# A hybrid encoder layer: another order inside the turns of its recurrence, and an order point for the first loads of the out projection

## The chip, the cores and the metric

The kernel runs on one core of one Trainium2 chip. The metric is the device time of one execution in microseconds (us). Three executions of the kernel before took 2543.28, 2548.71 and 2551.45 us; their median is 2548.71 us. A fourth execution was profiled, and all rows quoted here are from it.

The engines are named as in the profile: PE multiplies matrices (PEld loads its weights), ACT applies functions and copies out of the accumulator banks, DVE does element-wise arithmetic, POOL does smaller arithmetic, and SP only issues transfers.

## The reference, cut to what matters

One layer on x (2048 tokens, width 1024) and 256 memory tokens, all in float32, each step wrapped in RMS norms and added to a residual:

```python
z = u @ w_in                       # 2816 columns: 768 for attention, 4 x 512 for the recurrence
ya = swa_with_sinks(qa, ka, va)    # sliding window attention, 8 heads
yh = hgrn2(qh, fh, ih, gh)         # gated recurrence, 4 heads of 128 x 128 state
y  = concat(ya, yh) @ w_out        # the out projection
...
y  = cross_attention(u, m, wq_x, wk_x, wv_x, wo_x)
...
y  = (silu(u @ w_gate) * (u @ w_up)) @ w_down
```

The recurrence, chunk by chunk (64 tokens), is

```python
A     = (qc * exp(b - b_mid)) @ (kc * exp(b_mid - b)).T      # causal part within the chunk
o     = A @ vc + (qc * exp(b)) @ S_prev                      # plus what the state gives
S     = exp(b_last) * S_prev + (kc * exp(b_last - b)).T @ vc # the state for the next chunk
out   = rms_norm(o) * silu(g)
```

so the output of a chunk needs the state from before it, and the state from chunk to chunk is the only chain through time.

## The kernel before, in words

Every float32 product is made of three products of split operands (hi*hi, hi*lo, lo*hi), so each weight or activation tile is loaded raw by a transfer, split by ACT (hi) and DVE (lo), and then used by PE.

The layer runs in stages. First z is made for the first 1024 tokens. Then, in one stretch (`mix`), three strands run beside each other: the rest of the input projection, the attention, and the recurrence (`hgrn`). After that the *fold* (`fold_cross`) multiplies the cross attention's weights together ahead of time: eight steps for the keys, eight for the queries, eight for the values (`wv_x`, read in columns), and eight for the output weight (`wo_x`, read in rows). The eight `wo_x` tiles are numbered j = 0 to 7; each has 512 KB and feeds 12 matmuls of 512 columns into four accumulator banks, and two of them (one head) make two result tiles that go to `vo_d`. The raw tiles of the fold (`raw`) have three buffers. The last eight pairs of the recurrence run interleaved with the fold, two fold steps to a turn. Then come the blocked products of the rest of the layer (`phases`): the out projection (operand `y_d`), the scores, the values and the feed-forward part. Each of their blocks loads its operand as two tiles `sraw` of 512 KB, for which there are four buffers; block 0 of the out projection is the first.

The recurrence handles 128 tokens (a pair of chunks) with four helpers. `hgrn_front(n)` loads k, q and v of pair n, makes the masked A in one of two buffers `atz`, the scaled queries q6, and the transposes kt and vt. `hgrn_state` multiplies kt and vt and adds the decayed old state: POOL multiplies (L924), DVE adds (L925), into one of two buffers W. `hgrn_out` multiplies A by vt (L934) and the old W by q6 (L935), squares on ACT (L939), takes the root on POOL and scales on DVE (L944); it also loads the gate `sg`. `hgrn_last` transposes (L952), multiplies with the gate (L953) and stores to `y_d`. `hgrn` deals these out in turns; a turn handles the front of one pair and the rest of earlier ones.

What order the engines get: the program is traced in the order of the Python code, and a planner then plays it against a model of the engines at compile time, giving each engine, whenever it is free, the earliest traced instruction that is ready in that model. The order so found is fixed for each engine; on the chip each engine takes its instructions in that order and waits at each for its inputs. SP likewise issues its transfers one after the other. The buffers of one tag are given out in the order in which the program first writes them. `self.queued(ins)` adds a rule to the planner: what is traced inside on the engine of `ins` goes behind `ins` in that engine's order. It adds no wait. `self.traced(engine)` is the instruction traced last on an engine.

`phases` is a generator; the fold stage steps it nine times, which brings the first tiles T of the out projection's weights (loads into tiles named z, splits into T). Its tenth step calls `stream(0)`, which traces the two loads of block 0's operand (`sraw<-y_d`) and then yields. In the kernel before, this tenth step is part of the plain loop at the end of `mix`.

Of the kernel before, what the change touches and what calls it, by code (L numbers as in the profile page):

```python
# [48 lines left out]
class Layer:  # L49
# [79 lines left out]
    def raw_tile(self):  # L129
        self._n += 1  # L130
        return self.wp.tile([P, D], F32, tag="raw", name=f"raw_{self._n}", bufs=3)
# [62 lines left out]
    def mix(self):  # L194
        tc, I = self.tc, self.I
        kw = dict(reuse_waits="tile")
        with contextlib.ExitStack() as left:
# [40 lines left out]
            phases = self.phases(self.jobs(), None, lambda: self.io_tile("z"))  # L238
# [25 lines left out]
            with (  # L264
                tc.tile_pool(name="t3", bufs=3, **kw) as self.ts,
                tc.tile_pool(name="t4", bufs=3, **kw) as self.tb,
                tc.tile_pool(name="s3", bufs=2, side="right", **kw) as self.st_pool,
                contextlib.ExitStack() as at,
            ):
                self.banks(at, "ps3", **MOST)  # L270
                self.raws = 4
                for _ in phases:
                    pass

# [8 lines left out]
    def fold_cross(self):  # L283
# [10 lines left out]
        def split_tiles():  # L294

            if next(turn) % 3 < 2:
                return self.split_tiles()
            self._n += 1
            return [ph.tile([P, D], F32R, tag=f"w{x}", name=f"w{x}_{self._n}") for x in ("hi", "lo")]
# [18 lines left out]
        for t in range(M // P):  # L318
            m = raw_tile()
# [6 lines left out]
        for d in range(KT):  # L326
# [6 lines left out]
            o = self.io_tile("x")  # L333
# [12 lines left out]
        for h in range(4):  # L346
            banks = [[self.bank(k) for k in "sh"] for _ in range(2)]
            for i in range(2):
                j = 2 * h + i
                raw = raw_tile()  # L350
                self.load(raw, self.I["wo_x"][j * P:(j + 1) * P, :])
                wh, wl = split_tiles()
                self.split(raw, wh, wl, "A")
                for mt in range(2):
                    ms = slice(mt * P, (mt + 1) * P)
                    ah, al = vT[0][:, j, ms], vT[1][:, j, ms]
                    for q in range(2):
                        sl = slice(q * 512, (q + 1) * 512)
                        nc.tensor.matmul(banks[mt][q], ah, wh[:, sl], start=(i == 0), stop=False)
                        nc.tensor.matmul(banks[mt][q], ah, wl[:, sl], start=False, stop=False)  # L360
                        nc.tensor.matmul(banks[mt][q], al, wh[:, sl], start=False, stop=(i == 1))
                if i == 0:
                    yield
            for mt in range(2):
                o = self.io_tile("x")
                for q in range(2):
                    nc.scalar.activation(o[:, q * 512:(q + 1) * 512], banks[mt][q], AF.Copy)
                self.store(self.vo_d[(2 * h + mt) * P:(2 * h + mt + 1) * P, :], o)
            yield
# [547 lines left out]
    def hgrn_state(self, n, kinds, kt, vt):  # L917
        nc, ph = self.nc, self.hg
        prev = self.W
        W = self.W = ph.tile([P, 4, P], F32, tag="W", name=f"W{n}", bufs=2)  # L920
        ps = self.bank(kinds[0])
        for h in range(4):
            nc.tensor.matmul(ps[:, h * P:(h + 1) * P], kt[:, h, :], vt[:, h, :], start=True, stop=True)
        nc.gpsimd.tensor_tensor(W, prev, self.G[:, n, :, 1].unsqueeze(2).broadcast_to([P, 4, P]), ALU.mult)  # L924
        nc.vector.tensor_tensor(W, ps.rearrange("p (h t) -> p h t", h=4), W, ALU.add)  # L925

    def hgrn_out(self, n, kinds, q6, at, vt, W):
        nc, ph = self.nc, self.hg
# [28 lines left out]
    def hgrn(self, pairs, kinds):  # L957

        f, o = {}, {}
        for n in itertools.chain(pairs, (None, None)):  # L960
            if o:
                l, v = o.popitem()
                self.hgrn_last(l, kinds, *v)
            if f:
                m, (q6, at, kt, vt) = f.popitem()
                o[m] = self.hgrn_out(m, kinds, q6, at, vt, self.W)
                self.hgrn_state(m, kinds, kt, vt)
            if n is not None:
                f[n] = self.hgrn_front(n, kinds)
            yield  # L970

    def swa(self, pairs, kinds):
# [826 lines left out]
```

## Time and profile before

| | |
|---|---|
| median of three executions | 2548.71 us |
| the profiled execution: its time | 2551.48 us |
| the profiled execution: span of the program | 2549.8 us |
| PE busy in the span | 2504.8 us (98%) |
| DVE, ACT, POOL busy | 1794.9, 1261.8, 372.7 us |
| transfers | 482.13 MB, mean 189 GB/s |
| recurrence beside the fold and the input projection | about 600 to 730 us |
| last fold steps (`wo_x`) | 748 to 772 us |

The profile gives, for one execution, the start and length of each instruction, what it waited for, the clock that PE was granted (PEclk, 1.00 is full), and the transfers. A row of the timeline has start and length in us, engine, line, operation, output<-inputs, shapes, count, and in brackets the idle time just before it with what ended it. A row of a table by stretches gives for each engine the busy time and the instructions in the stretch, then the clock, the mean busy share of the 16 transfer engines and GB/s.

### The profile page before, as it was taken

What the parts mean: (1) busy time and instruction counts of PE and PEld (TensorE: products, weight loads), DVE (VectorE), ACT (ScalarE), POOL (GpSimd) and SP (SyncE); (2) the same over time, 40 slices, a digit from 0 to 9 for tenths busy, and PEclk for the clock granted to TensorE, in tenths of its full rate; (3) what the DMA queues carried; (4) which work ended last, traced back from release to release, by engine and by line L of the source; (5) the groups of instructions that cost most, each with busy time, mean ns of one, the idle gap of its engine ahead of it and who ended that gap; (6) DMA issues with size and microseconds to landing.
All of it is one profiled execution on the core that took longest, in us unless ns stands there. A gap on an engine that the chain in (4) does not pass through costs nothing.

```text
span 2549.8 us, 34301 instructions
## 1 busy us (share of the span) xinstructions
PE 2504.8 (98%) x12006; PEld 2094.9 (82%) x12006; DVE 1794.9 (70%) x2871; ACT 1261.8 (49%) x2635; POOL 372.7 (15%) x540
## 2 busy tenths in 40 slices
PE   9999999999999999999999999999999999999998
PEld 8878888888987778878878888888888888888886
DVE  8885588986466989887876655576566557574766
ACT  5553467664565566566753333353333335443543
POOL 4331334331301111102200000000000000000022
PEclk9999999999999999999999999999999999999999
DMA  6455645773887996866964522254566434565886
GB/s 200 148 166 178 187 146 152 219 233 101 263 296 265 319 328 192 268 206 220 331 209 140 182 91 84 75 206 143 163 207 198 142 118 160 177 191 106 229 174 154
DMA packets 379437, 482.13 MB, mean 189 GB/s; under 512 B 22016, under 2 KB 274944, under 8 KB 379264
## 3 DMA queue, kind: packets, MB, share of 16 engines
q1 hardware_dynamic: 373216, 457.92, 56.1%
q0 software_dynamic: 6048, 22.02, 5.1%
q8 instruction: 94, 1.54, 0.2%
q14 instruction: 79, 0.65, 0.1%
HBM read 313.14 MB, written 166.72 MB: 188 GB/s over the span
## 4 chain that ended last, share of the span: by engine, by line
PE 80%; DVE 7%; DMA 6%; ACT 3%; issue 3%; POOL 1%; SPq 1%; DVEq 0%; POOLq 0%; ACTq 0%
PE psm L1137 22%; PE psm L1139 22%; PE psm L1138 22%; PE psg L158 2%; PE psg L157 2%; PE psg L156 2%; DVE T L996 1%; DMA h1t_d<-row 1%; DVE S L996 1%; ACT junk L1512 1%; DMA raw<-in_wv_x_dram 1%; SPq L75 1%; DVE row L1406 1%; DVE sum L1112 0%; DMA qd<-z_d 0%
## 5 line engine op out<-in xcount | busy, mean ns | idle before, releaser
L1137 PE MATMUL psm<-T,S 128*128 128x512 f32 x2680 | 1034.7, 391 | 14.3 <-ACT part L1152 7.8
L1138 PE MATMUL psm<-T,S 128*128 128x512 f32 x2680 | 1043.0, 390 | 4.0 <-DVE T L996 3.9
L1139 PE MATMUL psm<-T,S 128*128 128x512 f32 x2680 | 1030.1, 390 | 4.4 <-DVE S L996 4.4
L1137 PEld LDWEIGHTS psm<-T,S 128*128 128x128 f32 x2680 | 503.5, 188 | 127.6 <-ACT part L1152 12.9
L1139 PEld LDWEIGHTS psm<-T,S 128*128 128x128 f32 x2680 | 503.5, 188 | 111.1 <-DVE S L996 6.6
L1138 PEld LDWEIGHTS psm<-T,S 128*128 128x128 f32 x2680 | 503.5, 188 | 110.0 <-DVE T L996 6.8
L993 ACT ACTIVATE S<-sum 128x512 fp32r<-128x512 f32 (+1 forms) x370 | 223.5, 619 | 378.1 <-PE psm L1139 276.3
L996 DVE TENSOR_TENSOR S<-sraw,S 128x512 fp32r<-128x512 f32 (+1 forms) x315 | 211.2, 678 | 212.4 <-ACT S L993 209.2
L1152 ACT ACTIVATE part<-psm 128x512 f32<-128x512 f32 x285 | 168.6, 596 | 249.5 <-PE psm L1139 231.6
L996 DVE TENSOR_TENSOR S<-sum,S 128x512 fp32r<-128x512 f32 (+1 forms) x388 | 257.2, 673 | 42.0 <-ACT S L993 38.3
L993 ACT ACTIVATE S<-sraw 128x512 fp32r<-128x512 f32 (+1 forms) x300 | 185.0, 618 | 113.1 <-PE psm L1139 110.3
L1545 POOL DMA_DIRECT2D y_d<-row x16 | 14.0, 877 | 1077.7 <-DVE row L1729 1026.8
L996 DVE TENSOR_TENSOR T<-row,T 128x1024 fp32r<-128x1024 f32 (+1 forms) x112 | 131.0, 1182 | 30.8 <-ACT T L993 28.7
L156 PE MATMUL psg<-u,whi 128*128 128x512 f32 x320 | 127.1, 397 | 0.8 <-DVE z L724 0.8
L158 PE MATMUL psg<-u,wlo 128*128 128x512 f32 x320 | 126.9, 397 | 0.0
L157 PE MATMUL psg<-u,whi 128*128 128x512 f32 x320 | 126.6, 396 | 0.0
L1512 ACT ACTIVATE junk<-row 128x512 f32<-128x512 f32 x160 | 99.5, 623 | 40.3 <-DVE row L1534 17.4
L993 ACT ACTIVATE T<-row 128x1024 fp32r<-128x1024 f32 (+1 forms) x112 | 113.3, 1031 | 5.7 <-DMA row<-d_s 3.5
L1680 DVE TENSOR_TENSOR row<-psm,part 128x512 f32<-128x512 f32 x66 | 43.7, 687 | 66.5 <-PE psm L1139 66.4
L1689 DVE TENSOR_TENSOR part<-psm,part 128x512 f32<-128x512 f32 x66 | 43.8, 687 | 60.5 <-PE psm L1139 60.3
L996 DVE TENSOR_TENSOR wlo<-raw,whi 128x1024 fp32r<-128x1024 f32 x44 | 53.8, 1223 | 44.6 <-ACT whi L993 29.5
L1729 DVE TENSOR_TENSOR row<-psm,part 128x512 f32<-128x512 f32 x72 | 49.1, 687 | 49.4 <-PE psm L1139 49.3
(362 smaller groups left out, 3584.7 us busy)
## 6 DMA issues: line engine op xcount, KB each, us to landing
sraw<-in_w_gate_dram SPq DMA_DIRECT2D x44, 512.0 KB, 3.9
sraw<-in_w_up_dram SPq DMA_DIRECT2D x44, 512.0 KB, 3.9
hid_d<-row SPq DMA_DIRECT2D x44, 512.0 KB, 2.7
sraw<-hid_d SPq DMA_DIRECT2D x32, 512.0 KB, 4.3
sraw<-in_w_in_dram SPq DMA_DIRECT2D x44, 256.0 KB, 3.8
z_d<-pair SPq DMA_DIRECT2D x20, 512.0 KB, 3.6
raw<-in_w_in_dram SPq DMA_DIRECT2D x20, 512.0 KB, 5.4
z_d<-z SPq DMA_DIRECT2D x20, 512.0 KB, 4.1
```

The lines of the kernel that those rows point to most:

```text
L156: nc.tensor.matmul(ps, ah, bh, start=(i == 0), stop=False)
L157: nc.tensor.matmul(ps, ah, bl, start=False, stop=False)
L158: nc.tensor.matmul(ps, al, bh, start=False, stop=(i == n - 1))
L993: self.nc.scalar.activation(hi, raw, AF.Copy)
L996: self.nc.vector.tensor_tensor(lo, raw, f32(hi), ALU.subtract)
L1137: nc.tensor.matmul(ps, s[:, 0, k, :], t[:, 0, k, :], start=st, stop=False, **kw)
L1138: nc.tensor.matmul(ps, s[:, 0, k, :], t[:, 1, k, :], start=False, stop=False, **kw)
L1139: nc.tensor.matmul(ps, s[:, 1, k, :], t[:, 0, k, :], start=False, stop=sp, **kw)
L1152: nc.scalar.activation(t, ps, AF.Copy)
L1512: self.nc.scalar.activation(junk, a, AF.Square, scale=float(D) ** -0.5, accum_out=to)
L1689: nc.vector.tensor_tensor(c, a, c, ALU.add)
L1729: nc.vector.tensor_tensor(d, a, b, ALU.add)
```

## The change

Two edits. In `hgrn`, a turn was traced as last (of pair l), output and state (of pair m), front (of pair n); now it is state (m), front (n), last (l), output (m). The output still uses the state from before pair m: `hgrn_state` returns it. Second, the tenth step of `phases` is taken inside `self.queued(self.folded)`, where `self.folded` is the load of the third `wo_x` tile (j = 2): the two loads of block 0's operand go behind that load in SP's order.

```diff
@@ mix
                 self.banks(at, "ps3", **MOST)
                 self.raws = 4
+                with self.queued(self.folded):
+                    next(phases)
                 for _ in phases:
                     pass
@@ fold_cross
                 raw = raw_tile()
                 self.load(raw, self.I["wo_x"][j * P:(j + 1) * P, :])
+                if j == 2:
+                    self.folded = self.traced(mybir.EngineType.SP)
                 wh, wl = split_tiles()
@@ hgrn_state
         nc.vector.tensor_tensor(W, ps.rearrange("p (h t) -> p h t", h=4), W, ALU.add)
+        return prev
@@ hgrn
         for n in itertools.chain(pairs, (None, None)):
+            if f:
+                m, (q6, at, kt, vt) = f.popitem()
+                W = self.hgrn_state(m, kinds, kt, vt)
+            else:
+                m = None
+            if n is not None:
+                f[n] = self.hgrn_front(n, kinds)
             if o:
                 l, v = o.popitem()
                 self.hgrn_last(l, kinds, *v)
-            if f:
-                m, (q6, at, kt, vt) = f.popitem()
-                o[m] = self.hgrn_out(m, kinds, q6, at, vt, self.W)
-                self.hgrn_state(m, kinds, kt, vt)
-            if n is not None:
-                f[n] = self.hgrn_front(n, kinds)
+            if m is not None:
+                o[m] = self.hgrn_out(m, kinds, q6, at, vt, W)
             yield
```

## The prediction, made before the result was known

> **What bounds the kernel now.** I read the page first, then the table by stretches over the part that the edits touch, then the list of PE's waits there, and last the timelines of SP, ACT, DVE and PE around the one wait that stands out.
>
> ```profile
> span 2549.8 us, 34301 instructions
> PE 2504.8 (98%) x12006; PEld 2094.9 (82%) x12006; DVE 1794.9 (70%) x2871; ACT 1261.8 (49%) x2635; POOL 372.7 (15%) x540
> 300.00:600.00 300.00, 296.03 (x1663) 253.97 (x1662) 259.58 (x627) 192.67 (x550) 100.32 (x156) 0.99 0.58 177
> 600.00:744.00 144.00, 143.07 (x1105) 137.42 (x1103) 75.49 (x109) 75.29 (x180) 35.30 (x44) 1.00 0.75 229
> 744.00:754.00 10.00, 6.16 (x21) 4.54 (x21) 6.13 (x9) 4.79 (x7) 0.00 (x0) 0.83 0.89 311
> 754.00:800.00 46.00, 46.00 (x202) 37.73 (x201) 18.38 (x20) 25.84 (x45) 2.53 (x3) 1.00 0.79 291
> 800.00:1300.00 500.00, 483.53 (x2154) 394.22 (x2153) 441.48 (x640) 313.70 (x698) 84.68 (x130) 1.00 0.84 269
> ```
>
> PE is the bound everywhere: it idles 2549.8 - 2504.8 = 45.0 us in the whole span. The edits leave PE's work as it is, so they can only win idle time, or add some. The recurrence runs between 300 and 730 us, where PE idles 300 - 296.03 = 3.97 us and 144 - 143.07 = 0.93 us. The ten microseconds from 744 stand out: 3.84 us idle and a clock of 0.83. Behind them, to 800 us, PE has no gap.
>
> ```profile
> 748.01 0.50 PE L359 MATMUL pss<-whi,kv 128*128 128x512 f32 x1 [3.54 <-ACT whi L993]
> 749.27 0.79 PE L360 MATMUL pss<-wlo,kv 128*128 128x512 f32 x1 [0.29 <-DVE wlo L996]
> 746.91 1.06 ACT L993 ACTIVATE whi<-raw 128x1024 fp32r<-128x1024 f32 x1 [1.80 <-DMA raw<-in_wo_x_dram]
> 736.25 10.58 DMA raw<-in_wo_x_dram
> 733.47 2.69 SPq L75 DMA_DIRECT2D sraw<-y_d  x4
> 736.25 4.86 SPq L75 DMA_DIRECT2D raw<-in_wo_x_dram  x3
> 743.77 1.58 SPq L75 DMA_DIRECT2D sraw<-y_d  x2
> 749.25 3.06 SPq L75 DMA_DIRECT2D raw<-in_wo_x_dram  x3
> 748.00:750.00 2.00, 1.69 (x5) 1.12 (x6) 1.95 (x2) 1.82 (x3) 0.00 (x0) 0.73 0.71 262
> 750.00:752.00 2.00, 2.00 (x7) 1.52 (x5) 1.96 (x3) 0.52 (x1) 0.00 (x0) 0.50 0.80 258
> 752.00:754.00 2.00, 2.00 (x9) 1.64 (x8) 0.00 (x0) 0.49 (x1) 0.00 (x0) 0.91 0.91 234
> ```
>
> The reader is to see a queue. PE waits 3.54 us for the first split of `wo_x`; that split waits for its load; the load was issued at 736.25 and took 10.58 us. Just ahead of it SP issued four `sraw<-y_d` of 512 KB (blocks 0 and 1 of the out projection), which nobody uses on PE before the fold ends at 772. Then the clock: it is at 0.50 to 0.91 while PE starts again, and the time lost is 2 x (0.27 + 0.50 + 0.09) = 1.72 us. The gap thus costs 3.54 + 0.29 + 1.72 = 5.55 us.
>
> **The change, part by part: the order point.** Both loads of block 0 go behind the third `wo_x` load. Buffers of one tag are given out in traced order, so block 1's and block 2's loads can't overtake block 0's: all six move, and with them 2 MB that stood ahead of the first `wo_x` tile. When are the three `wo_x` loads issued then? Each needs a raw buffer, freed by a split of `wv_x` on DVE.
>
> ```profile
> 734.36 1.22 DVE L996 TENSOR_TENSOR wlo<-raw,whi 128x1024 fp32r<-128x1024 f32 x1
> 735.91 1.23 DVE L996 TENSOR_TENSOR wlo<-raw,whi 128x1024 fp32r<-128x1024 f32 x1
> 739.52 1.23 DVE L996 TENSOR_TENSOR wlo<-raw,whi 128x1024 fp32r<-128x1024 f32 x1 [2.06 <-ACT whi L993]
> 738.43 1.06 ACT L993 ACTIVATE whi<-raw 128x1024 fp32r<-128x1024 f32 x1 [2.29 <-DMA raw<-in_wv_x_dram]
> 748.18 1.06 ACT L993 ACTIVATE whi<-raw 128x1024 fp32r<-128x1024 f32 x1 [0.21 <-DMA raw<-in_wo_x_dram]
> 744.00:748.00 4.00, 0.47 (x4) 0.27 (x3) 2.22 (x6) 1.96 (x3) 0.00 (x0) 1.00 1.03 399
> raw<-in_wo_x_dram SPq DMA_DIRECT2D x1, 512.0 KB, 4.0
> 752.39 0.39 PE L359 MATMUL psh<-whi,kv 128*128 128x512 f32 x1
> 752.62 0.39 PE L359 MATMUL pss<-whi,kv 128*128 128x512 f32 x1
> ```
>
> The splits end at 735.58, 737.14 and 740.75, so the first tile's load moves only from 736.25 to about 735.6. What moves more is its landing: nothing but the last `wv_x` tile is ahead of it, which lands by 738.43. A `wo_x` load issued without a queue took 4.0 us (the one of 749.25), and a full queue moves 399 GB/s, 524 KB in 1.31 us, also the step between the splits of the first two tiles (746.91, 748.18). So tile 0 lands at 735.6 + 4.0 = 739.6, tile 1 at 737.2 + 4.0 = 741.2, tile 2 at 740.8 + 4.0 = 744.8. ACT and DVE need about 1.06 + 1.23 us: tile 0 is split by 742. PE finishes the last `wv_x` product at 744.47 (0.47 us busy in the stretch from 744) and goes on at once: the 5.55 us go.
>
> What is late next is tile 3. SP issues the four `y_d` loads from 741.2 to 743.9 (2.69 us, as now), and tile 3 right behind; they land 1.31 us apart: 746.1, 747.4, 748.7, 750.0, and tile 3 at 751.3. Its halves are ready at 752.4 (hi) and 753.6 (lo). PE is there at 744.47 + 3 x 12 x 0.23 = 752.8, and starts with three hi products (0.7 us). So it just fits; tile 4 has its buffer free about 744 and lands one step later. The moved loads are themselves due by 772 and land by 750; their splits on ACT (0.63 us each) now fall among those of tiles 2 to 5 and the copies out of the banks. I put 0.5 us on that. Bounds: nothing lost (5.55 won) to the gap come back whole ahead of tile 3 (0 won); I take 5.0, near the upper end, because tile 3's row of sums fits without help. Blocks 1 and 2 have 20 us of cover and cost nothing; without it each late operand would cost its 1.31 us.
>
> **The turns.** Written out as a sequence, the order was last, output, state, front and is the same cycle after, begun at another place; no instruction is added. What changes is the distance: between the front of a pair and its output now lies a whole further turn, and between an output and the next state and front, which reuse its W, `atz`, q6 and vt buffers, nearly nothing where a turn lay.
>
> ```profile
> L924 POOL TENSOR_TENSOR W<-W,G 128x512 f32<-128x512 f32 x14 | 15.5, 1108 | 28.5 <-DVE W L925 26.7 <-DMA vr<-z_d 1.8
> L925 DVE TENSOR_TENSOR W<-psg,W 128x512 f32<-128x512 f32 x8 | 5.5, 688 | 9.2 <-PE psg L923 9.2
> PE pst L850 <- DVE w_mn L821: 0.9, 1, 0.9
> PE psg L156 <- DVE z L724: 0.8, 1, 0.8
> PE pss L158 <- DVE wlo L996: 0.8, 1, 0.8
> PE psh L859 <- ACT pth L854: 0.7, 2, 0.3
> PE psh L860 <- DVE ptl L855: 0.6, 1, 0.6
> PE psh L912 <- ACT atz L898: 0.3, 1, 0.3
> 592.00:596.00 4.00, 2.63 (x12) 1.89 (x13) 4.00 (x9) 3.23 (x13) 1.25 (x2) 0.92 0.27 75
> 596.00:600.00 4.00, 4.00 (x19) 3.42 (x18) 3.85 (x9) 2.77 (x5) 0.00 (x0) 0.66 0.53 191
> ```
>
> In the list of PE's waits from 300 to 730 one entry of eight belongs to the recurrence (L912, 0.3 us). PE has other work (projection, fold) whenever a turn is not ready; that work is the cover, and if it were gone each turn would show its own latency. POOL today multiplies the next W as soon as DVE has added the last (26.7 us of POOL's idle end with L925); after, L924 must also wait for L935 of the output just before. Behind L924 on POOL stand the next front's k and q products, and behind those PE's A. POOL has 35.30 of 144 us to do, so it can wait. Bounds: the gain can't be more than PE's idle there, 3.97 + 0.93 = 4.9 us; for the loss I take the nearest row, 0.3 us at each of 16 turns, 4.8 us. I take 0, between them, since nothing that PE waits for is moved nearer. SP's transfers in a turn (k, q, v, the gate, the store to `y_d`) keep their cycle too.
>
> **The sum.** 2551.48 - 5.0 + 0 = 2546.5 us for an execution like the profiled one, which stood 2.77 us over the median: 2543.7 us. Two things blur it. The planner starts anew from every shift, and the 16.47 us idle from 800 to 1300 are waits on ACT and DVE which another order may make a quarter more or less: 4 us. And the three times differ by 8 us; a difference of less than 0.3% (7.6 us) can hardly be told from none.
>
> **The rivals.** *More comes loose* (faster). The wait at L158 (0.8) is for the same crowded transfers, and the end of the attention from 592 to 600 costs 4 - 2.63 = 1.37 us and 4 x (0.08 + 0.34) = 1.68 us of clock. If a new order of the recurrence's DVE work takes both away: 2543.7 - 0.8 - 3.05 = 2539.9. For it: DVE is busy 4.00 of 4.00 there. Against it: most of that is the attention's own (L821, L855).
>
> *The stall moves to tile 3* (no change). If the planner also puts block 2's two loads ahead of tile 3, that is 2 x 1.31 = 2.6 us more; the lo half comes at 756.2, its use at 753.5, a stall of about 2.7 us and perhaps the slow clock again. Then 5.55 - 2.7 - 1.72 = 1.1 us are won: 2547.6. For it: at 743.77 SP sent those two ahead of tile 3 already now. Against: they need block 0's splits first, which come later.
>
> ```profile
> 1104.00:1108.00 4.00, 2.21 (x9) 1.52 (x8) 4.00 (x7) 4.00 (x7) 0.00 (x0) 0.92 0.93 369
> 1108.00:1112.00 4.00, 4.00 (x13) 3.12 (x13) 3.93 (x7) 2.67 (x5) 0.00 (x0) 0.66 0.00 0
> ```
>
> Whether a short stall costs clock: here PE lost 4 - 2.21 = 1.79 us and the clock fell to 0.66 all the same. The Trainium skill (TensorE: Matmul & The Clock Gate, Part 1) says that the clock halves after an idle window of about 3.4 us; by that a stall of 2.7 us would keep the clock, and this rival would give 2545.9. The row at 1108 speaks against it.
>
> *The short distance bites* (slower). In the eight turns beside the fold, the state right behind the output waits for it: L924 (1.04 us without its outlier, 1.11 in the mean) and L925 (0.69) in a row show on PE in each turn, 8 x 1.8 = 14.4 us, less the 5.0 won: 2558.1. It decides, that is it ends 0.3% over the time before, from (7.6 + 5.0) / 8 = 1.6 us a turn on. For it: two buffers each, and POOL in order. Against it: PE has two fold steps between one turn and the next.
>
> **How the numbers follow.** The forecast (gap gone, turns neutral; 2540 to 2548 by itself) has 0.50, more coming loose 0.20, the stall at tile 3 0.16, the short distance 0.14. Below 2541.1 (0.3%) lie nearly all of the second (0.19) and the lower third of the forecast (0.18): faster 0.37. Above 2556.3 lies most of the last (0.13), and 0.02 for a bad new order later: slower 0.15. The rest, 0.48, is no change that can be told. The range, 2537 to 2554, takes in the first three with the spread of the times and leaves out most of the fourth.
>
> **What would show it.** In the profile after: the first three loads `raw<-in_wo_x` ahead of `sraw<-y_d` on SP; PE without a gap over 0.5 us from 744 to 772 and the clock at 1.00 there; the fold over by about 766. The turns: PE's waits from 300 to 730 still near 5 us, with no L923, L896 or L935 of over 0.5 us among them. The prediction is wrong if a wait for `whi` appears at the fourth tile, if waits of POOL's L924 for L935 reach PE, or if the part behind 800 loses or wins more than 4 us.

## The result, and the profile after

In 18 executions each, the changed kernel took 2552.31 us in the median (2548.48 to 2556.48) and the kernel before, beside it, 2549.22 (2543.28 to 2551.45). The ratio is 1.0017, with a 95% interval of 1.0010 to 1.0023: 2.5 to 5.9 us slower. The forecast was 2543.7. The profiled execution took 2553.18 us, its span 2551.5. In the changed kernel the lines from the fold on are numbered 4 higher, those behind L925 mostly 5 to 8 higher (L859/L860 are now L863/L864, L952 is L957, L359 is L363).

The page of the changed kernel, span and first line of part 1:

```profile
span 2551.5 us, 34293 instructions
PE 2503.8 (98%) x12006; PEld 2091.0 (82%) x12006; DVE 1792.0 (70%) x2871; ACT 1260.8 (49%) x2635; POOL 367.1 (14%) x540
```

Its table by the stretches of the prediction:

```profile
300.00:600.00 300.00, 293.37 (x1653) 249.94 (x1652) 253.42 (x617) 189.27 (x553) 98.38 (x159) 1.00 0.59 176
600.00:744.00 144.00, 142.80 (x1094) 136.25 (x1093) 75.72 (x115) 74.72 (x180) 36.20 (x45) 1.00 0.71 216
744.00:754.00 10.00, 9.66 (x57) 8.07 (x55) 7.19 (x9) 5.72 (x10) 0.00 (x0) 1.00 0.80 269
754.00:800.00 46.00, 43.43 (x185) 34.35 (x186) 18.85 (x22) 25.77 (x45) 1.59 (x3) 1.00 0.87 336
800.00:1300.00 500.00, 482.99 (x2161) 394.10 (x2159) 440.75 (x639) 313.97 (x696) 85.33 (x131) 1.00 0.83 269
```

The reader is to see three things. From 300 to 600 us PE is busy 2.66 us less than before (296.03), and DVE 6.2 us less (259.58): work has slipped out of this stretch (some of PE's 2.66 us is the clock, which before had halved near 595). The hole from 744 to 754 is closed (9.66 us busy for 6.16, clock 1.00 for 0.83). And behind it, from 754 to 800, where PE had no gap, 2.57 us are now lost. Behind 800 little changes.

Where the shift begins is read from three rows of PE's timeline, before and after: the last transposes of the recurrence's first eight pairs, the attention's last product, and the fold's last product.

```profile
471.70 0.60 PE L952 MATMUL psh<-ident,on 128*128 128x128 f32 x4
...
602.56 0.48 PE L860 MATMUL psh<-ptl,vst 128*128 128x512 f32 x1
...
772.13 0.39 PE L361 MATMUL psh<-whi,kv 128*128 128x512 f32 x1
```

```profile
480.65 0.60 PE L957 MATMUL psh<-ident,on 128*128 128x128 f32 x4
...
606.36 0.48 PE L864 MATMUL psh<-ptl,vst 128*128 128x512 f32 x1
...
774.21 0.40 PE L365 MATMUL psh<-whi,kv 128*128 128x512 f32 x1
```

`ptl` and `vst` are operands of the attention, psh, pst and pss pairs of accumulator banks. The recurrence's first half ends 9.0 us later, the attention 3.8 us later; the fold ends only 2.1 us later, so some 1.7 us came back between. From the fold's end to the end of the span it is 1777.7 us before and 1777.3 after.

In the table below a run's landmarks are starts of PE instructions in its one profile: the last transpose of the recurrence's first half (471.70 above is the first of its group of four, 472.0 the last), the attention's last product, the last `wv_x` product, and the fold's last product. "Stretch" is the time from the wv_x landmark to the fold's.

| run | first half | attention | wv_x | fold | stretch | span |
|---|---|---|---|---|---|---|
| before | 472.0 | 602.6 | 744.2 | 772.1 | 27.9 | 2549.8 |
| after | 481.0 | 606.4 | 748.1 | 774.2 | 26.1 | 2551.5 |
| e1 order point alone | 472.6 | 603.1 | 744.1 | 770.2 | 26.1 | 2546.2 |
| e2 turns alone | 480.8 | 605.7 | 748.2 | 772.8 | 24.6 | 2550.0 |
| e3 turns, pairs 0 to 7 | 481.2 | 606.2 | 748.0 | 772.8 | 24.8 | 2548.6 |
| e4 turns, pairs 8 to 15 | 471.8 | 602.2 | 744.3 | 769.7 | 25.4 | 2549.5 |
| e5 point, splits behind tile 5 | 473.0 | 603.6 | 744.0 | 771.3 | 27.3 | 2547.6 |
| e9 point behind tile 5, splits behind 7 | 472.9 | 603.6 | 744.7 | 771.9 | 27.2 | 2551.1 |
| e13 as e9, half the bytes | 473.4 | 604.1 | 744.9 | 768.7 | 23.8 | 2546.6 |
| e14 before, half the bytes | 471.8 | 603.0 | 745.1 | 769.8 | 24.7 | 2545.1 |
| e6 as e3, three buffers | 480.8 | 606.3 | 747.4 | 774.0 | 26.6 | 2550.6 |
| e7 before, three buffers | 472.7 | 605.6 | 745.5 | 771.4 | 25.9 | 2548.2 |
| e8 as e3, two bank pairs | 483.3 | 615.8 | 755.7 | 782.6 | 26.9 | 2562.4 |
| e10 before, two bank pairs | 469.9 | 613.6 | 753.6 | 779.0 | 25.4 | 2554.1 |
| e11 last, state, front, output | 530.4 | 633.2 | 773.2 | 799.1 | 25.9 | 2581.3 |
| e12 state, last, output, front | 503.7 | 616.0 | 755.9 | 782.1 | 26.2 | 2562.4 |
| e15 new turns, then old | 479.5 | 610.3 | 750.9 | 777.7 | 26.8 | 2553.6 |
| e16 old turns, then new | 480.8 | 605.1 | 746.7 | 772.1 | 25.4 | 2550.0 |
| e17 before, two gate buffers | 472.0 | 603.6 | 743.7 | 766.7 | 23.0 | 2546.4 |
| e18 as e3, two gate buffers | 481.5 | 605.4 | 745.6 | 768.3 | 22.7 | 2545.3 |

Seven profiles have the old turns in the first half with nothing else changed there (before, e1, e4, e5, e9, e13, e14). Their attention ends from 602.2 to 604.1, 603.2 in the mean; up to 617 us every engine has the same instructions in the same order in all seven, so this is what executions differ by. After, e2 and e3, alike up to 620 us, have 605.7 to 606.4, 606.1 in the mean: 2.9 us later.

The stretch holds 3.4 us at half clock, 1.7 us of PE's time, in before, e1, e5 to e9, e11, e12 and e15, and none in the others. Without it that of before is 26.2 us, about as long as that of the changed kernel (26.1).

### The profile page after: what moved, and what is told of

The parts are those of the page before. It is cut to its first block, busy times and chain, and to the rows that moved or that the text cites. A ratio compares the mean times of both kernels' runs of the same rounds, so it can differ in the third digit from the quotient of the medians.

```text
span 2551.5 us, 34293 instructions
## 1 busy us (share of the span) xinstructions
PE 2503.8 (98%) x12006; PEld 2091.0 (82%) x12006; DVE 1792.0 (70%) x2871; ACT 1260.8 (49%) x2635; POOL 367.1 (14%) x540
## 4 chain that ended last, share of the span: by engine, by line
PE 51%; DVE 2%; DMA 1%; ACT 1%; issue 1%; POOL 0%; SPq 0%; DVEq 0%; POOLq 0%; ACTq 0%
PE psm L1147 17%; PE psm L1145 17%; PE psm L1146 17%; DVE T L1004 0%; ACT junk L1520 0%; PE pss L1406 0%; DVE S L1004 0%; DMA row<-d_s 0%; DMA out_dram<-row 0%; ACT T L1001 0%; DMA row<-in_w_down_dram 0%; DMA sraw<-in_w_gate_dram 0%; DMA row<-h_d 0%; DVE sum L1120 0%; ACT S L1001 0%
## 5 line engine op out<-in xcount | busy, mean ns | idle before, releaser
L156 PE MATMUL psg<-u,whi 128*128 128x512 f32 x320 | 128.6, 402 | 0.4 <-DVE z L728 0.4
L829 ACT ACTIVATE S<-S,w_mn 128x256 f32<-128x256 f32 (+1 forms) x128 | 63.0, 497 | 40.3 <-DVE w_mn L825 40.3
```

Source lines behind the costliest of these rows:

```text
L156: nc.tensor.matmul(ps, ah, bh, start=(i == 0), stop=False)
L829: nc.scalar.activation(s[:, r, o:], s[:, r, o:], AF.Exp, bias=mn[:, i:i + 1], scale=-1.0, accum_out=den[:, i:i + 1])
```

## The experiments: which part costs

e1 keeps the old turns and has the order point alone.

```diff
                 self.raws = 4
+                with self.queued(self.folded):
+                    next(phases)
...
```

> The order point alone, the recurrence's turns as before. Three theories of the 3 us lost by the whole change. BANKS: the new turns in the recurrence's first half (pairs 0 to 7) end their last output some 10 us later, the attention's second half gets the shared accumulator banks later and PE runs out of cover at its end (3.8 us); the order point by itself wins about 2 us of the 5.55 us gap and loses the rest to new short stalls. ORDER POINT: the order point itself loses 3 us, since the moved loads crowd the transfers from 745 to 770 us, and the turns are neutral, as predicted. SHORT DISTANCE: the turns beside the fold (pairs 8 to 15) lose. BANKS and SHORT DISTANCE: 1 to 4 us faster than before, no wait of 3.5 us on PE near 745 us, the attention's last matmul at 602 to 603 us as before. ORDER POINT: 2 to 4 us slower than before.

e2 has the turns alone, as in the change.

> The new turns alone, without the order point. BANKS: 3 to 5 us slower than before, the attention's last matmul near 606 us against 602.6, the gap of 3.5 us near 748 us still there (shifted). ORDER POINT: within 1.5 us of before. SHORT DISTANCE: 3 to 5 us slower, with the attention's end where it was and the loss between 606 and 745 us.

e3 and e4 have the new turns in one half of the recurrence only (`kinds` is "h" in the first half; e4 has `!=` there):

```diff
         f, o = {}, {}
+        if kinds == "h":
...
+            return
         for n in itertools.chain(pairs, (None, None)):
```

> The new turns for pairs 0 to 7 only (beside the attention), the old ones for pairs 8 to 15, no order point. BANKS: the whole loss of the turns, 3 to 5 us slower than before, attention's last matmul near 606 us. SHORT DISTANCE and ORDER POINT: within 1.5 us of before.

> The new turns for pairs 8 to 15 only (beside the fold), the old ones for pairs 0 to 7, no order point. BANKS and ORDER POINT: within 1.5 us of before, everything up to 600 us the same. SHORT DISTANCE: 3 to 5 us slower, PE waiting for the recurrence between 606 and 745 us.

Each was timed 11 times beside 33 executions of before. e1: ratio 1.0001 (0.9992 to 1.0010), no change, and so neither the gain of BANKS nor the loss of ORDER POINT. e2: 1.0012 (1.0003 to 1.0021), 3.1 us slower, most of the change's loss (1.0017 is 4.3 us). The wait of 3.5 us that BANKS had there is gone. e3: 1.0012 (1.0002 to 1.0021), the same again. e4: 1.0005 (0.9995 to 1.0015), no change that can be told. So the turns beside the attention cost; for those beside the fold no loss is shown, though up to 3.8 us isn't excluded: from the attention's end to the last `wv_x` product it is 141.6 us before and 142.1 in e4.

The loss stands in the times; the profiles show only where it may arise. The spans of e2 and e3 are 2550.0 and 2548.6 us beside 2549.8 before; the profiled execution of before stood 2.3 us over its median, with three stretches of halved clock, near 595, 749 and 1107 us. At the fold's end e2 and e3 are only 0.7 us late.

## The experiments: why the order point is worth so little

PE's wait of 3.54 us is gone wherever the point is set. In e1 another takes its place. ACT's timeline, and PE's, of e1:

```profile
742.82 0.37 ACT L316 ACTIVATE kv<-pss 128x256 fp32r<-128x256 f32 x1
746.30 1.15 ACT L997 ACTIVATE S<-sraw 128x512 fp32r<-128x512 f32 x2 [3.12 <-DMA sraw<-y_d]
747.36 1.04 ACT L997 ACTIVATE whi<-raw 128x1024 fp32r<-128x1024 f32 x1
748.31 0.61 ACT L997 ACTIVATE S<-sraw 128x512 fp32r<-128x512 f32 x1
748.83 0.36 ACT L316 ACTIVATE kv<-psh 128x256 fp32r<-128x256 f32 x1
```

```profile
750.65 0.50 PE L363 MATMUL psh<-whi,kv 128*128 128x512 f32 x1 [2.13 <-DVE kv L317]
...
752.30 0.63 PE L365 MATMUL psh<-whi,kv 128*128 128x512 f32 x1
```

The loads of block 0 have moved, its splits (`S<-sraw`) have not: ACT, in order, waits 3.12 us for the moved load while the split of the third `wo_x` tile and the copy that ends the `wv_x` products (`kv`) stand behind it. PE then waits 2.13 us for that copy, and a product takes 0.63 us where 0.39 is usual: the clock is halved for 3.4 us, as it was before. e5 moves the splits too:

```diff
+                with self.queued(*self.folded2):
+                    for _ in range(2):
+                        next(phases)
...
+                if j == 5:
+                    self.folded2 = [self.traced(mybir.EngineType.Activation), self.traced(mybir.EngineType.DVE)]
```

> The old turns and the order point, and with it the splits of block 0's operand on ACT and DVE, put behind ACT's and DVE's splits of the sixth wo_x tile (j = 5). UNMOVED SPLITS (the order point takes PE's wait away, but ACT then waits for block 0's loads ahead of the splits of later wo_x tiles and of the copies out of the banks: 3.12 us at 746.3 in the run of the order point alone): without them ahead no PE wait of over 0.8 us between the last wv_x product and the fold's end; this stretch goes from 26.1 us (order point alone; 27.9 before) to 23 to 24.5; the fold ends 4 to 5.5 us earlier than before's 772.1, and 3.5 to 5 us are won, ratio 0.998 to 0.9987. TRANSFERS (the rival: 16 queues are full from 738 to 768 in any order, so that the late tiles come late whoever is first): the stretch stays at 25.5 to 26.5 us, with waits for the splits of tiles 5 to 7 in place of the one near 750, and at most 2 us are won.

Ratio 1.0011 (1.0001 to 1.0021; 12 executions beside 17): no gain, if anything a loss. PE's timeline of e5:

```profile
752.79 0.51 PE L368 MATMUL pss<-whi,kv 128*128 128x512 f32 x1 [0.86 <-ACT whi L1002]
...
758.68 0.50 PE L368 MATMUL pss<-whi,kv 128*128 128x512 f32 x1 [2.12 <-ACT x L376]
```

Tile 3 now comes 0.86 us late, and the splits, let in behind tile 5, stand ahead of copies out of the banks. e9 puts the loads behind tile 5's and the splits behind tile 7's (the lines of e5 are those with a minus).

```diff
-                if j == 2:
+                if j == 5:
...
-                if j == 5:
+                if j == 7:
```

> Old turns; block 0's loads behind the load of the sixth wo_x tile (j = 5) and its splits on ACT and DVE behind those of the eighth (j = 7). In e5 tile 3's split still waited for its load, which stood behind the four loads of y_d (landed at 751.58, a wait of 0.86 us on PE), and block 0's splits (five of 0.54 us at 755.45) stood ahead of the copies out of the banks of head 1 (a wait of 2.12 us on PE). PLACE (what the order point is worth is set by what its loads and splits are put ahead of): with both places mended the stretch from the last wv_x product to the fold's end is 22 to 24 us (27.9 before, 26.1 order point alone), no PE wait of over 0.8 us in it, 3 to 5 us won, ratio 0.998 to 0.9988. FULL QUEUES (the rival: the transfers around 740 to 768 are as many as fit, and a late block 0 makes PE wait at the start of the out projection instead): the stretch is short too, but a wait of 1.5 us or more for S or sraw comes up right behind the fold, and under 1.5 us are won by 800 us.

Ratio 1.0006 (0.9997 to 1.0014). PLACE falls: the first six tiles are in time, and now tile 6 is late. FULL QUEUES, as put there, misses too: the stretch isn't short, and no wait comes up behind the fold. For the next two runs the name stands for too many bytes in the stretch. They keep all work of the engines and halve the bytes of the `wo_x` tiles, leaving out half of the output weight; on SP e13 has e9's order and e14 that of the kernel before.

```diff
-                self.load(raw, self.I["wo_x"][j * P:(j + 1) * P, :])
+                self.load(raw[:, 0:512], self.I["wo_x"][j * P:(j + 1) * P, 0:512])
...
+                twice = raw[:, 0:512].unsqueeze(1).broadcast_to([P, 2, 512])
```

> As e9, but each wo_x tile loads only its left 512 columns (256 KB) and the splits read them twice, so that PE, ACT and DVE do the same work with half the bytes; the right half of the output weight is left out, and the result is not the layer's. FULL QUEUES (the order only chooses which of the late loads PE meets: 8 loads of wo_x, 4 of y_d and 8 stores to vo_d, 20 times 1.28 us are 25.6 us of transfers beside 22 us of PE's work): 5.1 us less of transfers, the stretch from the last wv_x product to the fold's end goes from 27.2 to 22 to 23 us, without a wait of over 0.8 us. PLACE (another in-order wait is to blame): the stretch stays at 26 us or more.

> The same halved loads in the kernel before, without the order point; the same half is left out. FULL QUEUES: the first wo_x load still stands behind the four loads of y_d and its wait stays at 2 to 3.5 us, but nothing is late behind it: the stretch is 24 to 26.5 us, and so the order point is worth 2 to 4 us once there are fewer bytes, where it was worth 1.8 with all of them. PLACE: the wait and the stretch stay as before (3.5 and 27.9).

PE's timeline of e9, and of e13, the longest wait in the stretch:

```profile
764.07 0.50 PE L368 MATMUL pss<-whi,kv 128*128 128x512 f32 x1 [2.41 <-ACT whi L1002]
```

```profile
763.26 0.50 PE L370 MATMUL pss<-wlo,kv 128*128 128x512 f32 x1 [0.53 <-DVE wlo L1006]
```

With half the bytes the same order has no long wait, and the stretch is 23.8 us for 27.2 (1.7 of the 3.4 us are the halved clock behind e9's wait). e14's stretch is 24.7 for 27.9, as FULL QUEUES had it (here too 1.7 of the 3.2 us are clock); but the point is worth only 0.9 us between the two, less than the 2 to 4 expected. So PE pays in this stretch for transfers that come late, and the order point chooses which tile pays. What it does to them is read from the table by stretches, before and after:

```profile
737.00:744.00 7.00, 7.00 (x61) 7.00 (x61) 4.75 (x8) 4.74 (x8) 0.00 (x0) 1.00 1.03 373
...
754.00:772.00 18.00, 18.00 (x79) 14.55 (x78) 6.12 (x5) 11.44 (x19) 0.00 (x0) 1.00 0.72 269
```

```profile
737.00:744.00 7.00, 7.00 (x60) 6.92 (x59) 5.27 (x7) 4.45 (x6) 0.00 (x0) 1.00 0.97 324
...
754.00:772.00 18.00, 15.43 (x62) 11.25 (x63) 8.12 (x8) 12.59 (x20) 0.00 (x0) 1.00 0.95 379
```

Before, the 16 transfer engines were 0.72 busy in the last 18 us of the fold and PE never waited there. After, they are 0.95 busy and PE loses 2.57 us. SP's timeline, the waits of PE there, and ACT's timeline of the changed kernel show the rest:

```profile
739.21 6.61 SPq L75 DMA_DIRECT2D raw<-in_wo_x_dram  x3
745.91 1.41 SPq L75 DMA_DIRECT2D sraw<-y_d  x3
748.29 0.34 SPq L75 DMA_DIRECT2D raw<-in_wo_x_dram  x1
748.68 0.53 SPq L75 DMA_DIRECT2D sraw<-y_d  x1
```

```profile
PE pss L363 <- ACT x L371: 1.3, 1, 1.3
PE pss L363 <- ACT whi L1001: 0.7, 1, 0.7
PE pss L364 <- DVE wlo L1004: 0.5, 1, 0.5
```

```profile
753.62 1.15 ACT L1001 ACTIVATE S<-sraw 128x512 fp32r<-128x512 f32 x2 [1.31 <-DMA sraw<-y_d]
754.68 0.58 ACT L371 ACTIVATE x<-pss 128x512 f32<-128x512 f32 x1
...
768.11 1.06 ACT L1001 ACTIVATE whi<-raw 128x1024 fp32r<-128x1024 f32 x1 [0.21 <-DMA raw<-in_wo_x_dram]
```

The first three `wo_x` loads go ahead of `y_d`, as the change wants. The 1.3 us is again a split of block 0 ahead of a copy out of the banks. The other two are both for tile 6, its hi and then its lo half: its load went out at 759.04 and landed at 766.76, where 757.49 and 762.12 were the times before.

Two more facts take the point's gain away. With the new turns in the second half, SP's fixed order already has the first `wo_x` load ahead of the four of `y_d`, with no rule. SP's timeline of e2:

```profile
739.00 0.34 SPq L75 DMA_DIRECT2D raw<-in_wo_x_dram  x1
739.43 1.92 SPq L75 DMA_DIRECT2D sraw<-y_d  x4
```

So in the changed kernel there was no long wait to remove; against e2 the point makes the stretch longer (26.1 for 24.6). And e1's profile, 1.9 us ahead at the fold's end, didn't show in its times: its executions had a mean granted clock of 0.9965, those of before 0.9975. In these executions of before alone, 0.001 of clock goes with 1.4 us (1.5 and 2.4 in the executions of before beside e9 and e5); where the slow stretches of e1's other executions lay isn't known.

## The experiments: why the turns cost

The first thought was that the state and the next front now wait for the output just before them, or that the last output holds the bank pair psh that the attention's later tiles also use. e6 gives W, q6, vt and the masked A a third buffer (below, W's), e7 is its control; e8 keeps the attention off psh (the second pair of lines), e10 is its control.

```diff
-        W = self.W = ph.tile([P, 4, P], F32, tag="W", name=f"W{n}", bufs=2)
+        W = self.W = ph.tile([P, 4, P], F32, tag="W", name=f"W{n}", bufs=3)
...
-                swa = self.swa(range(NT), lambda n: "st" if n < NPB else "sth")
+                swa = self.swa(range(NT), lambda n: "st")
```

> The new turns in the first half (as in e3), with three buffers in place of two for what an output reads and the next state and front write: W, q6, vt and the masked A. SHORT DISTANCE (the state's POOL multiplication and the next front wait until the output just before has been multiplied; in e3 POOL's multiplication starts 2.0 us behind the output in 4 of 5 turns): the last of the first half comes back from 481.2 to 474 or less, and attention's end from 606.2 to 602 to 603.5. BANKS or the LONGER TAIL (after the last state two more uses of the two psh banks, 9 us each, are to be made, whatever the buffers): the last of the first half at 479 or later, attention's end at 605 or later.

> The control for e6: the old turns with the same three buffers. If the buffers alone do something the turns are not the reason: SHORT DISTANCE and BANKS both expect no change here, attention's end at 602 to 603, the last of the first half at 471 to 473.

> The new turns in the first half (as in e3), with the attention kept off the bank pair psh that the recurrence's first half uses (from its ninth tile on it takes its banks from three pairs, here from two throughout). BANKS (the last output and the last transposes of the first half hold psh until 481, and attention's tiles 8 to 10 wait for it): attention's end comes back by 2 us or more against e3's 606.2, and its tenth tile's first scores from 472.8 to under 468. LATENESS OF DVE (5.7 us less of DVE's work is done by 600 in e3 than before, whatever the banks): attention's end stays at 605 or later, or is later still because it has one bank pair less.

> The control for e8: old turns, attention on two bank pairs throughout. If attention's end comes at 610 or later here too, the missing bank pair costs it by itself, and e8 (615.8) says nothing for shared banks as the cause; the distance to e8 is then what the new turns cost without any shared bank: over 3 us (LATENESS OF ENGINES) or under 1.5 us (CHANCE OF THE ORDER: the planner finds another order from any edit, and attention's end moves by as much as with the three buffers of e7, 602.6 to 605.6).

SHORT DISTANCE falls: e6 is as late as e3 (480.8 and 606.3). BANKS falls as the whole cause: without shared banks both orders are some 10 us later, and the new one still 2.2 us behind the old, between the 1.5 and the 3 us that were to decide. But e7, which no theory wanted to move, moved by 2.4 us against the mean of 603.2. So an edit that leaves the turns alone can move the attention's end by almost as much as the change does; and against e7 e6 is only 0.7 us late, so that the buffers may still be a part of the cause.

e11 and e12 change the order within the first half's turn in other ways, e11 and then e12 (the conditions around these lines stay as in the change):

```diff
+                self.hgrn_last(l, kinds, *v)
+                W = self.hgrn_state(m, kinds, kt, vt)
+                f[n] = self.hgrn_front(n, kinds)
+                o[m] = self.hgrn_out(m, kinds, q6, at, vt, W)
```

```diff
+                W = self.hgrn_state(m, kinds, kt, vt)
+                self.hgrn_last(l, kinds, *v)
+                o[m] = self.hgrn_out(m, kinds, q6, at, vt, W)
+                f[n] = self.hgrn_front(n, kinds)
```

> First half only: last, state, front, output, so that only the output and the state have moved against each other's front (the output is behind the front, the last stays first). OUTPUT BEHIND THE FRONT: attention's end at 605 to 607, the last of the first half at 479 or later, as in e3. LAST BEHIND THE FRONT: attention's end at 602 to 603.5. CHANCE OF THE ORDER: anywhere between 602 and 607, without relation to e12.

> First half only: state, last, output, front, so that only the state is moved ahead (the output still comes ahead of the front, with the old state handed on). OUTPUT BEHIND THE FRONT: attention's end at 602 to 603.5, the last of the first half at 471 to 474. STATE FIRST (what costs is POOL's and DVE's state work ahead of the output): attention's end at 605 or later. CHANCE OF THE ORDER: anywhere between 602 and 607.

Both are far worse, 30 and 13 us at the attention's end. OUTPUT BEHIND THE FRONT misses in both. STATE FIRST holds in e12 by its letter (605 or later), and all orders that put the state ahead of the output are late, the change's, e11's and e12's; but 13 us where the change loses 3 says that it isn't the state alone. This rival was not followed further. In both the turns themselves get longer. The front of pair 1 to that of pair 7 takes 23.9 us a turn before, 24.8 in e3, 27.4 in e12 and 31.1 in e11. The end of the attention follows that of the recurrence: 472, 481, 504 and 530 go with 602.6, 606.2, 616.0 and 633.2. e15 and e16 switch the order at the seventh turn (`i` counts the turns; e16 has `i >= 6`).

```diff
+                if i < 6:
+                    W = self.hgrn_state(m, kinds, kt, vt)
...
+                else:
+                    self.hgrn_last(l, kinds, *v)
...
```

> First half: the new turns up to the sixth, the old ones from the seventh on, so that the outputs catch up ahead of the last two fronts. TAIL (with the new turns the output lags a front behind, and the last two outputs with their transposes come behind the last front with nothing beside them: last of the first half at 481 for 472, which holds up the attention that shares the engines and the bank pair): last of the first half at 471 to 475, attention's end at 602 to 604. STEADY TURNS (every turn costs, through the waits of ACT and POOL for the output just before): last of the first half at 474 or later, attention's end at 605 or later. CHANCE OF THE ORDER: neither, above all an attention's end that does not follow the last of the first half.

> First half: the old turns up to the sixth, the new ones from the seventh on; only the last two fronts run with the output behind them. TAIL: last of the first half at 479 to 483, attention's end at 605 to 607, all of the loss. STEADY TURNS: at most a third of it, attention's end at 602.5 to 604. CHANCE OF THE ORDER: an attention's end that does not follow the last of the first half.

PE's timeline of e16, the rows of the first half's last transposes and of the attention's end, and those of e15:

```profile
480.52 0.60 PE L953 MATMUL psh<-ident,on 128*128 128x128 f32 x4
...
605.14 0.48 PE L860 MATMUL psh<-ptl,vst 128*128 128x512 f32 x1
```

```profile
479.18 0.60 PE L953 MATMUL psh<-ident,on 128*128 128x128 f32 x4
...
610.26 0.48 PE L860 MATMUL psh<-ptl,vst 128*128 128x512 f32 x1
```

e16 meets TAIL: only the last two fronts have the output behind them, and the whole delay of the recurrence's end is there, with 1.9 of the 2.9 us at the attention's. e15 misses TAIL and meets STEADY TURNS: its recurrence ends no earlier, since the turn of the switch takes 34 us from front to front, and its attention ends later than in either order.

The traces part the two strands. The recurrence's delay is its tail: the last front begins at 442.2 us before, at 441.2 in e3 and at 439.6 in e16, and from there to the last transpose it is 29.8, 40.0 and 41.2 us. The attention's delay is not the tail alone. Its copies `vst` for the eighth tile, on ACT, start at 419.1 before and at 423.4 in e3 (419.7 in e16), when the last front hasn't begun; those for the tenth at 464.2, 475.6 and 465.0, those for the eleventh at 490.0, 502.5 and 495.4. So in e3 the steady turns delay the attention ahead of any tail, and in e16, where two turns are new, it falls behind only with the tail. Most of either delay is made good by the attention's end.

A fourth pair, with two buffers for the gate and the scaled output, asks for the size of chance:

```diff
-        sg = ph.tile([P, 4, P], F32, tag="sg", name=f"sg{n}")
+        sg = ph.tile([P, 4, P], F32, tag="sg", name=f"sg{n}", bufs=2)
...
```

> Old turns, with two buffers in place of one for the gate sg and the scaled output on. No theory needs these buffers. If attention's end moves by under 1 us from 602.6, an edit that should do nothing does nothing here, and e7's 3.0 us (602.6 to 605.6) come from its buffers; if it moves by 2 us or more, CHANCE OF THE ORDER is as large as the whole loss of the change.

> The new turns in the first half with the same two buffers. A fourth pair of old and new (602.6 and 606.2 as they are, 605.6 and 606.3 with three buffers, 613.6 and 615.8 on two bank pairs). TAIL: the new turns are later than e17 by 2 to 4 us, the last of the first half by 8 to 11 us. CHANCE OF THE ORDER: the difference of attention's ends is under 1 us or has the other sign.

e17's attention is at 603.6, inside the spread of the old turns; e18's is 1.8 us later. Over the four pairs (plain, three buffers, two bank pairs, two gate buffers) the new turns end the recurrence's first half 9, 8, 13 and 9.5 us later, and the attention 2.9, 0.7, 2.2 and 1.8 us later. The sign is the same each time; the size is about what e7 moved without any change of the turns.

How such a delay reaches PE is seen in ACT's timeline around 420 us, before and in e3:

```profile
419.05 0.22 ACT L799 ACTIVATE vst<-pss 128x64 fp32r<-128x64 f32 x1
```

```profile
421.58 0.27 ACT L898 ACTIVATE atz<-psh 64x128 f32<-64x128 f32 x1 [3.49 <-DVE atz L897]
...
423.43 0.22 ACT L799 ACTIVATE vst<-pss 128x64 fp32r<-128x64 f32 x1 [0.17 <-PE pss L797]
```

In e3 ACT waits 3.49 us for a step of the recurrence, and the attention's copy `vst` stands behind it, 4.4 us later than before. PE doesn't idle then; it takes the input projection instead. That cover is used up early: of the projection's first products (L156) PE makes 162 from 300 to 500 us before and 167 after, and from 500 to 600 us 88 before and 81 after. In the table by stretches, before and after, and in the list of the changed kernel's waits of PE from 300 to 640 us:

```profile
500.00:600.00 100.00, 97.30 (x507) 81.40 (x508) 87.96 (x227) 60.16 (x172) 23.95 (x39) 0.98 0.65 202
```

```profile
500.00:600.00 100.00, 93.79 (x495) 76.78 (x494) 85.82 (x231) 62.23 (x182) 24.64 (x42) 1.00 0.62 193
```

```profile
PE psh L864 <- DVE ptl L859: 3.4, 2, 2.1
```

PE is busy 3.51 us less in these 100 us, 80 us behind the wait of ACT (before had its clock of 0.98 there, 1.7 us, which the change doesn't have). What it then waits for is above all the attention's own operand `ptl`, 3.4 us (0.6 before, from the prediction's list); e3 has 3.1. That the delayed attention and the spent cover make these waits fits all rows and is argued, not shown; what part is the steady turns, what part the tail, and what part the chance of another fixed order stays open.

e17 and e18 brought something nobody looked for: their stretches are 23.0 and 22.7 us, the shortest of all, without an order point. SP's timeline of e17, and the table by stretches of e18:

```profile
729.29 3.33 SPq L75 DMA_DIRECT2D sraw<-y_d  x4
732.72 5.31 SPq L75 DMA_DIRECT2D raw<-in_wo_x_dram  x3
```

```profile
737.00:744.00 7.00, 7.00 (x62) 7.00 (x61) 5.18 (x8) 5.54 (x10) 0.00 (x0) 1.00 1.04 402
744.00:754.00 10.00, 9.78 (x50) 7.97 (x50) 6.50 (x9) 7.58 (x10) 0.00 (x0) 1.00 0.94 342
754.00:772.00 18.00, 18.00 (x80) 14.62 (x79) 6.98 (x7) 9.17 (x16) 0.00 (x0) 1.00 0.72 275
```

The loads of `y_d` go 4.2 us earlier than before (733.47), the `wo_x` loads 3.5 us earlier, and PE's longest wait is 0.31 us in e17 and 0.23 in e18. All bytes are there; they went earlier, into the time of the `wv_x` products. One execution each took 2548.14 and 2547.03 us beside one of before of 2550.78; more were not run, so a gain isn't shown.

## Why the prediction was wrong, by its steps

**The order point, 5.0 us won.** Right: the three loads go ahead, PE goes on at once behind the last `wv_x` product, and the slow clock at that place is gone. The term that failed is the "0.5 us" for the moved loads' splits and what they meet. The step "so it just fits" looked at tile 3 alone and at landing times alone. Those were good: tiles 0 to 3 landed at 739.1, 741.8, 744.6 and 751.8 us in e1, within 0.6 us of the forecast. But tile 3 did not fit: it landed at 751.6 in e5, PE was there at 751.9, not at 752.8, and waited 0.86 us. It left out two things: the splits did not move with the loads, and stand in ACT's order ahead of work that PE needs (2.13 us in e1, 1.3 us after), and the transfers behind tile 3 come later, as the first come earlier (tile 6 after, 0.7 and 0.5 us). Measured, 1.8 us of the stretch for the point alone, none of it in the times (within -2.0 and +2.5 us); and with the new turns a loss of 1.5. The sum added two edits as if each met the kernel before; the second removed the wait by itself.

**The turns, 0.** This is the step that turned the sign: "nothing that PE waits for is moved nearer". The measured term is +3.1 us (0.8 to 5.4), inside the bounds (-4.9 to +4.8), but the reason was wrong twice. As predicted, no wait of PE on the recurrence's own lines appeared. But the step looked only at what PE waits for in the old order, not at what is taken later: ACT and DVE give the attention its turn later, 11 us later at the tenth tile, and PE's waits for the attention's `ptl` in psh grow from 0.6 to 3.4 us. And the cover was taken to be there throughout; from 500 to 600 us PE has fewer products of the input projection left. Why the new order delays the attention stays open (steady turns, tail, the state's place or chance).

**The rivals.** *The short distance* was looked for in the eight turns beside the fold; there it wasn't seen (e4), and in the first half, where the loss is, more buffers didn't take it away (e6). *The stall moves to tile 3* was the nearest in kind: it moved, to the copy behind block 0's splits in e1, to tile 3 and the copies in e5, to tile 6 in e9, to the copies and tile 6 after. *More comes loose* had the attention's end lose its idle time; the idle time grew.

**The blur.** The part behind the fold moved by 0.4 us in the profiles, within the 4 allowed. The range held the time, and the outcome given the largest chance, no change that can be told at 0.3%, came in; both by the width of the range, since the time moved up where 5 us down was forecast.

**The clock.** The trace of before had the clock fall after 1.79 us of idle time; the Trainium skill (TensorE: Matmul & The Clock Gate, Part 1) has a window of about 3.4 us for it. Here a wait of 2.13 us (e1), one of 2.12 (e5) and one of 1.79 (e7, behind the `wv_x` products) were followed by a halved clock. But length alone doesn't decide: the waits of 2.39 us at that place in e10 and e16 were followed by none, nor was this one of the changed kernel, from PE's timeline.

```profile
523.53 0.50 PE L864 MATMUL psh<-ptl,vst 128*128 128x512 f32 x1 [2.07 <-DVE ptl L859]
```

## What to carry to other kernels

A load that is put later must have its consumers put later with it, on every engine that takes its instructions in a fixed order; otherwise the wait moves from the queue of transfers into that engine (e1). That alone is not enough (e5, e9). Before moving a transfer, count the bytes on both sides: one that leaves a full stretch for one that is nearly full moves the stall, and the time to look for is earlier. An edit of the order in a stretch where PE is covered can be paid where the cover runs out, so ask what each strand does later, not only who waits now; and measure each part of a change both alone and beside the other.

## What the hardware showed that was not expected

A step of ACT's queue that waited 3.12 us for a transfer cost PE more than half the wait that the transfer's move had saved. Stretches of 3.4 us at half clock, 1.7 us of PE's time each, came in most profiles: three in that of before, none in that of the changed kernel, nine in e11's, two of them twice as long (the last microseconds of each kernel are left aside). Some places come back, near 595, 820 and 1107 us, but not in every profile. They are a part of why the times of one kernel spread over 8 us (2543.28 to 2551.45), and a gain of 2 us in one profile, like e1's, need not be in the median.
